# Weights that stand still: products of 512 and of 256 columns in turn, or in two groups

## The chip, the cores and the metric

The kernel runs on one core of a Trainium2 chip. Its time is the device time of that core in microseconds (us). The core has five engines that run side by side and wait for one another through semaphores: TensorE (matrix products; PE in the profile, its weight loads PEld), VectorE (DVE), ScalarE (ACT), GpSimd (POOL) and SyncE (SP, which issues most transfers). A product on TensorE has a stationary operand of 128 x 128, which a weight load brings in, and a moving operand that streams past it, here 512 or 256 columns wide. The result is added up in a bank of PSUM, which holds 512 float32 columns.

## The reference

One layer of a hybrid block for 256 tokens, with a context of 256 more, model width 2048. Both token sets are normalised and modulated, and multiplied with one wide matrix `w_in` (2048 x 19456), whose columns are cut into the inputs of two branches and their gates:

```python
xn = rmsnorm(h, norm_gain[l]) * (1.0 + scale) + shift
cn = rmsnorm(hc, norm_gain[l]) * (1.0 + scale_c) + shift_c
aq, ak, av, ag, hq, hff, hfb, hi, hg, ma, mb = split_columns(xn @ w_in[l])
```

The attention branch uses aq, ak, av with the context's keys and values and is gated by `silu(ag)`. The other branch is a gated recurrence over time in two directions: hff and hfb give its forget gates (also for the context, which gives the states to start from), hq its queries (through silu), hi its values, hg its output gate. Both are projected (`w_o_hgrn`, `w_o_attn`), merged with sigmoid gates from ma and mb, projected by `w_out`, added to x and normalised. All of it is float32.

## The kernel before

Each float32 factor is split into a high part, rounded to TensorE's float32r, and a low part, the remainder. A product of two such numbers is taken as high x high + high x low + low x high, three products on TensorE.

The weights come in chunks of 128 x 1024. SyncE transfers a chunk into `raw`, ScalarE makes the high part `wh` from it (L85, or L635 in the quad stage), VectorE the low part `wl` (L86, L636). `wh` and `wl` have three buffers each. In two places the weights are the stationary operand and the tokens move:

- `quad_col` (L639 to L685) computes the forget gates' columns for x and context. It is run 13 times and saves work by seven products of combined blocks in place of eight: `combos` forms combinations of four weight blocks on VectorE (L616), `token_sums` has formed those of the tokens (S) before. Each of the seven makes one chunk: eight products with the high part of the weights, whose moving operand is 512 columns, the high and the low part of the tokens side by side (L660), and then eight with the low part of the weights and 256 columns, the high part of the tokens (L663). All sixteen go into one bank; the low products add to its first 256 columns. A copy or a sum by ScalarE and VectorE (L667 to L679) takes the bank's content out behind the sixteenth.
- `proj_col_x_g` (L147 to L159) computes 256 columns for x alone (the recurrence's queries, the attention's gates). It goes through the 2048 rows in four chunks. A chunk has again eight products of 512 columns with the weights' high part (L154), then eight of 256 columns with the low part (L157), in turn over two banks. It is run 16 times: 64 chunks.

Everywhere else on this path (L100 to L103, L732 to L737) the tokens are stationary and the weights move.

TensorE's order is the order of the code in both stages (`manual_schedule`). The other engines' orders are set by a planner with modelled times, within the priorities that the code gives; the splits and the copies out of the banks have a high one. Around `proj_col_x_g`, the function `weave` lays the steps of the recurrence (`pair`) on TensorE between the chunks; it counts the columns that each chunk reports.

Of the kernel before, what the change touches and what calls it, by code (L numbers as in the profile page):

```python
# [16 lines left out]
T = 256  # L17
KT = D // P
# [20 lines left out]
def block_kernel(ctx: ExitStack, tc: tile.TileContext, x, c, cx, c_ctx, w_ada, b_ada, norm_gain, w_in,  # L39
                 b_merge, lb_f, lb_b, hg_gain, w_oh, sink, w_oa, w_out, fin_gain, cst, msk, out):  # L40
    nc = tc.nc
    pe, act, dve, pool = nc.tensor, nc.scalar, nc.vector, nc.gpsimd
# [18 lines left out]
    def wload(w, row0, nk, col0, ncol, rp=None):  # L61

        raw = (rp or wp).tile([P, 1024], F32, tag="raw", name="raw", bufs=8 if rp else 5)
        rv = raw[:, : len(col0) * nk * ncol].rearrange("p (g k c) -> p g k c", g=len(col0), k=nk)
        for g, co in enumerate(col0):
            nc.sync.dma_start(rv[:, g], w[row0: row0 + nk * P, co: co + ncol].rearrange("(k p) c -> p k c", p=P))
        return raw, rv
# [10 lines left out]
    def wchunk(w, row0, nk, col0, ncol):  # L78
        cl = col0 if isinstance(col0, tuple) else (col0,)
        raw, rv = wload(w, row0, nk, cl, ncol)  # L80
        h = wp.tile([P, 1024], F32R, tag="wh", name="wh", bufs=3)
        lo = wp.tile([P, 1024], F32R, tag="wl", name="wl", bufs=3)
        n = len(cl) * nk * ncol
        with tc.high_priority(PRIO):
            last_hi[0] = act.activation(h[:, :n], raw[:, :n], AF.Copy).ins  # L85
            last_lo[0] = dve.tensor_tensor(lo[:, :n], raw[:, :n], h[:, :n].bitcast(F32), op=ALU.subtract).ins  # L86
        parts = [(h[:, g * nk * ncol: (g + 1) * nk * ncol].rearrange("p (k c) -> p k c", k=nk),
                  lo[:, g * nk * ncol: (g + 1) * nk * ncol].rearrange("p (k c) -> p k c", k=nk)) for g in range(len(cl))]
        return parts if isinstance(col0, tuple) else parts[0]
# [15 lines left out]
    def bank(name="pj"):  # L105
        return pj.tile([P, 512], F32, tag="pj", name=name)

    def proj_tok_g(w, col0, src, toks):
# [7 lines left out]
            yield len(toks) * 6 * 512  # L116
        return banks

    def result(g):

        while True:
            try:
                next(g)
            except StopIteration as e:
                return e.value

    def proj_tok(*a):
        return result(proj_tok_g(*a))
# [18 lines left out]
    def proj_col_x_g(w, col0):  # L147

        banks = [bank() for _ in range(2)]
        for k0 in range(0, KT, 4):  # L150
            h, lo = wchunk(w, k0 * P, 4, col0, 256)
            parts = [(banks[i], slice(i * P, (i + 1) * P), j) for j in range(4) for i in range(2)]
            for o, cs_, j in parts:
                pe.matmul(o.rearrange("p (a t) -> p a t", a=2), h[:, j, cs_], xHL[:, :, k0 + j, :T],  # L154
                          start=k0 + j == 0, stop=False)
            for o, cs_, j in parts:
                pe.matmul(o[:, :T], lo[:, j, cs_], xH[:, k0 + j, :T], start=False, stop=k0 + j == KT - 1)  # L157
            yield 24 * T
        return banks  # L159

# [16 lines left out]
    xHL = base.tile([P, 2, KT, 512], F32R, tag="xHL", name="xHL")  # L177
    xH, xL = xHL[:, 0], xHL[:, 1]
# [60 lines left out]
    with pl("st", reuse_waits="tile") as st:  # L239
# [153 lines left out]
        def first_highs(u, n):  # L393

            tg, nb = FIRST[u % 3]
            f = [wp.tile([P, 1024], F32R, tag=tg_, name=tg_, bufs=3)[:, : n * 512] for tg_ in ("wh", "wl")]
            qt = fp.tile([P, 2, 512], F32R, tag=tg, name="wq", bufs=nb)
            q = [qt[:, r, : n * 256] for r in range(2)]
            for hl, raw in zip((f, q), raws[u]):
                act.activation(hl[0], raw, AF.Copy)  # L400
            fv = [a.rearrange("p (k c) -> p k c", k=n) for a in f]
            chunks[u] = [[a[:, :, :256] for a in fv], [a.rearrange("p (k c) -> p k c", k=n) for a in q],
                         [a[:, :, 256:] for a in fv]]
            return [lambda hl=hl, raw=raw: dve.tensor_tensor(hl[1], raw, hl[0].bitcast(F32), op=ALU.subtract)
                    for hl, raw in zip((f, q), raws[u])]
# [54 lines left out]
        with tc.manual_schedule(engines={mybir.EngineType.PE, mybir.EngineType.SP, mybir.EngineType.Activation,  # L460
                                         mybir.EngineType.DVE}):
            unit = modulation(*UNITS[0])
            for i in range(4):
                rest(8)
                take(unit, 1)
                if i == 1:
# [6 lines left out]
            first = [(bank(), bank()), (bank(), bank()),  # L473
                     tuple(ps.tile([P, 512], F32, tag=tg, name="pf") for tg in ("o", "al2"))]

            plan = {0: 2, 2: 3, 3: 9}
            for u, (k, n) in enumerate(UNITS):
                lows = first_highs(u, n)
# [26 lines left out]
    def bank8():  # L505

        i = turn8[0] % 8
        turn8[0] += 1
        return bank() if i < 4 else ps.tile([P, 512], F32, tag=("tp", "o", "al1", "al2")[i - 4], name="pm")

    def half(a, h):

        return a.rearrange("p (a h t) -> p a h t", a=2, h=2)[:, :, h, :]

    def pairs_of(a):
        return a.rearrange("p (a t) -> p a t", a=2)
# [44 lines left out]
    with pl("sp", reuse_waits="tile") as sp:  # L561
# [49 lines left out]
        def combos(b):  # L611


            def sub(o, x_, y_):
                with tc.high_priority(PRIO):
                    dve.tensor_tensor(o, x_, y_, op=ALU.subtract)  # L616

            t = tmp()
            yield b["11"]
            sub(t, b["12"], b["11"])  # L620
            yield t
            sub(t, b["22"], t)
            yield t
            yield b["22"]
            sub(b["12"], b["22"], b["12"])
            yield b["12"]
            yield b["21"]
            sub(t, b["21"], t)
            yield t
# [9 lines left out]
        def quad_col(d, h0):  # L639

            co = (C_FF, C_FB)[d] + h0 * HD
            b = {n: wload(w_in, 1024 * (n[0] == "2"), 8, (co + HD * (n[1] == "2"),), HD)[0]
                 for n in ("11", "12", "22", "21")}
            m_ = [bank8() for _ in range(3)]
            into = {0: (0, True), 1: (1, True), 2: (0, False), 3: (1, False), 4: (0, False), 5: (2, True), 6: (0, False)}
            sg = [base.tile([P, 512], F32, tag="sm", name="sg", bufs=3) for _ in range(2)]
            s15 = fp.tile([P, 2, 512], F32, tag="F1", name="s15")
            su = None

            def joined(m, s, dst):  # L650


                dve.tensor_tensor(s, m, s, op=ALU.add)
                dve.tensor_tensor(dst, pairs_of(s[:, :T]), pairs_of(s[:, T:]), op=ALU.add)

            for (i, _, mv), src in zip(ORDER, combos(b)):
                h, lo = [a.rearrange("p (k c) -> p k c", k=8) for a in two(src)]
                z, fresh = into[i]
                for k in range(8):
                    pe.matmul(m_[z].rearrange("p (z a t) -> p z a t", z=2, a=2), h[:, k, :], mv(k),  # L660
                              start=fresh and k == 0, stop=False, skip_group_check=True)
                for k in range(8):
                    pe.matmul(pairs_of(m_[z][:, :T]), lo[:, k, :], mv(k)[:, 0], start=False, stop=k == 7,  # L663
                              skip_group_check=True)
                with tc.high_priority(2 * PRIO):
                    if i < 2:
                        act.activation(s15[:, i, :], m_[i], AF.Copy)  # L667
                    elif i == 2:
                        su = base.tile([P, 512], F32, tag="bb", name="su", bufs=2)
                        act.activation(su, m_[0], AF.Copy)  # L670
                    elif i == 3:
                        joined(m_[1], su, half(sg[1], 0))
                    elif i == 4:
                        joined(m_[0], s15[:, 1, :], half(sg[1], 1))
                    elif i == 5:
                        joined(m_[2], s15[:, 0, :], half(sg[0], 0))
                    else:
                        act.activation(half(sg[0], 1), pairs_of(m_[0][:, T:]), AF.Copy)
                        dve.tensor_tensor(half(sg[0], 1), pairs_of(m_[0][:, :T]), half(sg[0], 1), op=ALU.add)  # L679
            F = fp.tile([P, 2, 512], F32, tag="F0", name="F0", bufs=2)  # L680
            for i in (1, 0):
                act.activation(sg[i], sg[i], AF.Sigmoid)
                act.activation(F[:, i, :], sg[i], AF.Identity, scale=lbc[:, 2 + d, h0 + i: h0 + i + 1],
                               bias=lbc[:, d, h0 + i: h0 + i + 1])
            nc.scalar.dma_start(F_dr[d][h0 // 2], F.rearrange("p i t -> p (i t)"))  # L685
# [774 lines left out]
    for n in range(3):  # L1460
        bo = [bank() for _ in range(2)]
        for k0 in range(0, KT, 2):
            h, lo = wchunk(w_out, k0 * P, 2, n * 512, 512)
# [8 lines left out]
    for k0 in range(0, KT, 4):  # L1472
        h, lo = wchunk(w_out, k0 * P, 4, D - 512, 256)
# [85 lines left out]
```

## Time and profile before

| | |
|---|---|
| median of 3 runs | 1584.49 us (1583.45 to 1588.19) |
| profiled execution | 1586.59 us, its span 1584.8 us |
| TensorE busy | 1561.6 us, 99% of the span |
| VectorE busy | 1201.5 us, 76% |
| ScalarE busy | 860.5 us, 54% |
| GpSimd busy | 142.1 us, 9% |
| granted TensorE clock | 0.999 |
| products, and weight loads | 10954 each |
| quad stage (`quad_col`) | from 440 to 699 us |
| woven stage (`proj_col_x_g` among others) | from 695 to 1252 us |

Times in the views are microseconds from the span's start, unless marked ns. A row of the timeline has the start, the time from the first start to the last end, the engine, the line of the code, the operation, the tiles it writes and reads, and how many instructions were merged. A row of the groups has the count, the busy time, the mean of one in ns, and the idle time before them. Ends of products on TensorE are modelled and overlap the next one's start, so that paces are read from starts. A row of the waits says who waited for whom, the total, how often, and the longest. A row of the chain of waits has the start, the time that it held the chain, and what it was.

### The profile page before, as it was taken

How to read it: one execution, taken by the hardware profiler on the slowest of the kernel's cores; microseconds unless marked ns; L12 is line 12 of the kernel's file. 1: busy time of each engine (PE TensorE's matmuls, PEld its weight loads, DVE VectorE, ACT ScalarE, POOL GpSimd, SP SyncE). 2: the span in 40 equal slices, each digit the busy share in tenths (PEclk: the TensorE clock that was granted, in tenths of full speed). 3: DMA queues.
4: the chain of work that ended last, by engine and by line, in shares of the span. 5: the costliest groups of instructions: out<-in, count | busy, mean ns of one | idle time of the engine just before them, and what ended most of it. 6: DMA issues, size and time to landing. Idle time of an engine off the chain costs nothing. (4 is left out here: it accounts for less than half of the span.)

```text
span 1584.8 us, 27868 instructions
## 1 busy us (share of the span) xinstructions
PE 1561.6 (99%) x10954; PEld 1343.8 (85%) x10954; DVE 1201.5 (76%) x1764; ACT 860.5 (54%) x1344; POOL 142.1 (9%) x280
## 2 busy tenths in 40 slices
PE   7999999999999999999999999999999999999998
PEld 4568899999988888888888888888888888888887
DVE  4449977777787878878888897888878777757764
ACT  4336443333355555566656666575666776744442
POOL 2000000000000000011212222121121000000000
PEclk9999999999999999999999999999999999999999
DMA  9996734434444444467777877878677854458661
GB/s 366 386 387 230 226 111 130 134 132 134 133 147 127 134 130 137 136 225 252 243 247 244 300 260 233 270 243 273 221 261 249 289 159 154 155 180 295 226 197 69
DMA packets 242900, 333.83 MB, mean 211 GB/s; under 512 B 12080, under 2 KB 162000, under 8 KB 242000
## 3 DMA queue, kind: packets, MB, share of 16 engines
q1 hardware_dynamic: 214096, 249.54, 48.5%
q0 software_dynamic: 19168, 64.08, 11.8%
q10 hardware_dynamic: 9504, 18.42, 3.2%
q8 instruction: 86, 1.41, 0.4%
q14 instruction: 46, 0.38, 0.1%
HBM read 300.53 MB, written 31.47 MB: 209 GB/s over the span
## 5 line engine op out<-in xcount | busy, mean ns | idle before, releaser
L85 ACT ACTIVATE wh<-raw 128x1024 fp32r<-128x1024 f32 x284 | 298.8, 1059 | 236.3 <-PE pj L101 151.7
L86 DVE TENSOR_TENSOR wl<-raw,wh 128x1024 fp32r<-128x1024 f32 x284 | 344.0, 1219 | 89.9 <-ACT wh L85 88.9
L100 PE MATMUL pj<-wh,xHL 128*128 128x512 f32 (+1 forms) x768 | 298.6, 390 | 0.0
L101 PE MATMUL pj<-wh,xHL 128*128 128x512 f32 (+1 forms) x768 | 294.8, 385 | 0.0
L103 PE MATMUL pj<-wl,xHL 128*128 128x512 f32 (+1 forms) x768 | 202.7, 385 | 0.0
L635 ACT ACTIVATE wh<-T 128x1024 fp32r<-128x1024 f32 x75 | 79.5, 1060 | 166.8 <-DVE T L616 83.9
L100 PEld LDWEIGHTS pj<-wh,xHL 128*128 128x128 f32 x768 | 144.4, 188 | 28.2 <-ACT sg L219 0.6
L101 PEld LDWEIGHTS pj<-wh,xHL 128*128 128x128 f32 x768 | 144.5, 188 | 27.6
L103 PEld LDWEIGHTS pj<-wl,xHL 128*128 128x128 f32 x768 | 142.0, 188 | 28.9
L635 ACT ACTIVATE wh<-raw 128x1024 fp32r<-128x1024 f32 x100 | 105.3, 1055 | 71.9 <-PE pj L734 23.7
L154 PE MATMUL pj<-xHL,wh 128*128 128x512 f32 x512 | 130.3, 396 | 0.0
L636 DVE TENSOR_TENSOR wl<-raw,wh 128x1024 fp32r<-128x1024 f32 x100 | 121.8, 1218 | 9.8 <-ACT wh L635 9.7
L636 DVE TENSOR_TENSOR wl<-T,wh 128x1024 fp32r<-128x1024 f32 x75 | 91.5, 1220 | 32.8 <-ACT wh L635 32.8
L154 PEld LDWEIGHTS pj<-xHL,wh 128*128 128x128 f32 x512 | 92.4, 189 | 16.9
L157 PEld LDWEIGHTS pj<-xHL,wl 128*128 128x128 f32 x512 | 69.8, 190 | 5.2
L204 DVE SCALAR_TENSOR_TENSOR acc<-hgw,cg,acc 128x512 f32<-128x512 f32 x60 | 44.9, 748 | 35.0 <-DMA hgw<-in_w_ada_dram 35.0
L157 PE MATMUL pj<-xHL,wl 128*128 128x256 f32 x512 | 71.3, 282 | 0.0
L912 DVE TENSOR_TENSOR A<-A,X 128x512 f32<-128x512 f32 x96 | 61.6, 682 | 0.1
L616 DVE TENSOR_TENSOR T<-raw,T 128x1024 f32<-128x1024 f32 x50 | 60.9, 1218 | 0.1
L616 DVE TENSOR_TENSOR raw<-raw 128x1024 f32<-128x1024 f32 x25 | 30.6, 1225 | 36.7 <-DMA raw<-in_w_in_dram 36.7
L541 POOL DMA_DIRECT2D hgw<-in_w_ada_dram x64 | 35.0, 547 | 235.3 <-DVE acc L204 157.6
L660 PE MATMUL pj<-S,wh 128*128 128x512 f32 x208 | 52.6, 395 | 1.6 <-ACT s L667 1.6
(353 smaller groups left out, 3155.1 us busy)
## 6 DMA issues: line engine op xcount, KB each, us to landing
raw<-in_w_in_dram SPq DMA_DIRECT2D x300, 512.0 KB, 4.6
raw<-in_w_ada_dram SPq DMA_DIRECT2D x64, 512.0 KB, 8.0
hgw<-in_w_ada_dram POOLq DMA_DIRECT2D x64, 256.0 KB, 4.5
raw<-in_w_o_hgrn_dram SPq DMA_DIRECT2D x32, 512.0 KB, 3.6
raw<-in_w_o_attn_dram SPq DMA_DIRECT2D x32, 512.0 KB, 4.1
raw<-in_w_out_dram SPq DMA_DIRECT2D x28, 512.0 KB, 4.1
F<-F POOLq DMA_DIRECT2D x16, 512.0 KB, 7.2
F<-F ACTq DMA_DIRECT2D x13, 512.0 KB, 4.4
```

The costliest lines, as they stand in the source:

```text
L85: last_hi[0] = act.activation(h[:, :n], raw[:, :n], AF.Copy).ins
L86: last_lo[0] = dve.tensor_tensor(lo[:, :n], raw[:, :n], h[:, :n].bitcast(F32), op=ALU.subtract).ins
L100: pe.matmul(o, s[0], m[0], start=first, stop=False)
L101: pe.matmul(o, s[1], m[0], start=False, stop=False)
L103: pe.matmul(o, s[0], m[1], start=False, stop=last)
L154: pe.matmul(o.rearrange("p (a t) -> p a t", a=2), h[:, j, cs_], xHL[:, :, k0 + j, :T], start=k0 + j == 0, stop=False)
L157: pe.matmul(o[:, :T], lo[:, j, cs_], xH[:, k0 + j, :T], start=False, stop=k0 + j == KT - 1)
L616: dve.tensor_tensor(o, x_, y_, op=ALU.subtract)
L635: act.activation(h, src, AF.Copy)
L636: dve.tensor_tensor(lo, src, h.bitcast(F32), op=ALU.subtract)
L660: pe.matmul(m_[z].rearrange("p (z a t) -> p z a t", z=2, a=2), h[:, k, :], mv(k), start=fresh and k == 0, stop=False, skip_group_check=True)
L912: dve.tensor_tensor(av, av, f.unsqueeze(3).to_broadcast([P, 2, n2, b]), op=ALU.mult)
```

## The change

Both places issue the same products with the same operands into the same banks. Their order within a chunk is another: a new function `in_turn` puts a few high products first (four in `proj_col_x_g`, three in `quad_col`), then a low and a high in turn until the highs are used up, then the lows that are left. For three first the order of the sixteen is HHH LH LH LH LH LH LLL.

```diff
+    def in_turn(highs, lows, lead):
+
+        order = [highs.pop(0) for _ in range(lead)]
+        for hi, lo in zip(highs, lows):
+            order += [lo, hi]
+        return order + lows[len(highs):]
+
@@ proj_col_x_g
             parts = [(banks[i], slice(i * P, (i + 1) * P), j) for j in range(4) for i in range(2)]
-            for o, cs_, j in parts:
-                pe.matmul(o.rearrange("p (a t) -> p a t", a=2), h[:, j, cs_], xHL[:, :, k0 + j, :T],
-                          start=k0 + j == 0, stop=False)
-            for o, cs_, j in parts:
-                pe.matmul(o[:, :T], lo[:, j, cs_], xH[:, k0 + j, :T], start=False, stop=k0 + j == KT - 1)
+            highs = [(o.rearrange("p (a t) -> p a t", a=2), h[:, j, cs_], xHL[:, :, k0 + j, :T], k0 + j == 0, False)
+                     for o, cs_, j in parts]
+            lows = [(o[:, :T], lo[:, j, cs_], xH[:, k0 + j, :T], False, k0 + j == KT - 1) for o, cs_, j in parts]
+            for o, w_, m, first, last in in_turn(highs, lows, 4):
+                pe.matmul(o, w_, m, start=first, stop=last, skip_group_check=True)
             yield 24 * T
@@ quad_col
-                for k in range(8):
-                    pe.matmul(m_[z].rearrange("p (z a t) -> p z a t", z=2, a=2), h[:, k, :], mv(k),
-                              start=fresh and k == 0, stop=False, skip_group_check=True)
-                for k in range(8):
-                    pe.matmul(pairs_of(m_[z][:, :T]), lo[:, k, :], mv(k)[:, 0], start=False, stop=k == 7,
-                              skip_group_check=True)
+                highs = [(m_[z].rearrange("p (z a t) -> p z a t", z=2, a=2), h[:, k, :], mv(k), fresh and k == 0, False)
+                         for k in range(8)]
+                lows = [(pairs_of(m_[z][:, :T]), lo[:, k, :], mv(k)[:, 0], False, k == 7) for k in range(8)]
+                for o, w_, m, first, last in in_turn(highs, lows, 3):
+                    pe.matmul(o, w_, m, start=first, stop=last, skip_group_check=True)
```

A high is a product with the weights' high part and 512 columns, a low one with their low part and 256 columns.

## The prediction, on record before the changed kernel ran

> **What bounds the kernel now.** I read the page first, for the engines' shares.
>
> ```profile
> span 1584.8 us, 27868 instructions
> ...
> PE 1561.6 (99%) x10954; PEld 1343.8 (85%) x10954; DVE 1201.5 (76%) x1764; ACT 860.5 (54%) x1344; POOL 142.1 (9%) x280
> ...
> L154 PE MATMUL pj<-xHL,wh 128*128 128x512 f32 x512 | 130.3, 396 | 0.0
> ...
> L157 PE MATMUL pj<-xHL,wl 128*128 128x256 f32 x512 | 71.3, 282 | 0.0
> ```
>
> TensorE is busy for 99% of the span, so what counts is the pace at which it takes its products. The change touches L154/L157 (512 products each) and L660/L663. How many of the latter there are, the groups kept apart by shape tell:
>
> ```profile
> L660 PE MATMUL pj<-S,wh 128*128 128x512 f32 x208 | 52.6, 395 | 1.6 <-ACT s L667 1.6
> L660 PE MATMUL pm<-S,wh 128*128 128x512 f32 x208 | 52.5, 394 | 0.7 <-ACT s L667 0.7
> L660 PE MATMUL pj<-xHL,wh 128*128 128x512 f32 x160 | 40.1, 392 | 0.0
> L660 PE MATMUL pm<-xHL,wh 128*128 128x512 f32 x152 | 38.0, 392 | 0.0
> ```
>
> That makes 728 = 91 chunks of 8 highs (512 columns) and 8 lows (256 columns), beside 64 chunks of L154/L157. The durations in these rows (about 395 and 282 ns) overlap and are no pace. The pace comes from starts, so next I took TensorE's timeline. Five whole chunks of the quad stage, first and last row:
>
> ```profile
> 487.83 2.00 PE L660 MATMUL pj<-S,wh 128*128 128x512 f32 x8
> ...
> 501.80 0.40 PE L660 MATMUL pm<-S,wh 128*128 128x512 f32 x1
> ```
>
> A chunk takes 13.97 / 5 = 2.794 us, so the 155 chunks take 433 us, 27% of the span. A difference of 0.3% of the run (4.75 us, about what a measurement of this kernel can tell from no change) would need 0.031 us per chunk.
>
> What would a chunk take if each product ran at its steady pace? For 512 columns I take a stretch that has only these (24 products lie between the two starts), for 256 columns likewise (24 again):
>
> ```profile
> 1454.68 0.39 PE L100 MATMUL pj<-wh,xHL 128*128 128x512 f32 x1
> ...
> 1460.12 0.39 PE L100 MATMUL pj<-wh,xHL 128*128 128x512 f32 x1
> ```
> ```profile
> 399.80 0.28 PE L732 MATMUL pj<-wh,xHL 128*128 128x256 f32 x1
> ...
> 402.68 0.28 PE L732 MATMUL pm<-wh,S 128*128 128x256 f32 x1
> ```
>
> That is 5.44 / 24 = 0.2267 us and 2.88 / 24 = 0.120 us. Eight of each make 2.773 us; the chunk of today is 0.021 us above that. The chain of waits shows where the surplus sits:
>
> ```profile
> 893.06 1.81 PE pj L154 x8
> 894.87 0.95 PE pj L157 x8
> 895.83 1.84 PE pj L154 x8
> ```
>
> The first eight highs follow other products of 512 columns and take 1.81; the next eight follow lows and take 1.84. Turning from lows back to highs thus costs about 0.02 to 0.03 us, once per chunk, and nothing else in the chunk is lost: no wait stands there.
>
> **The change part by part.** The same 16 products per chunk are issued, with the same weight loads, no DMA, no copy, no new tile. What moves is the order: quad chunks go HHH, then five times LH, then LLL; L154 chunks go HHHH, four times LH, LLLL. There are four things to price.
>
> *First, the loads.* Each product loads its own weights. If the loads of the lows set their pace, mixing in the highs would hide them. Products of 128 columns show the pace of loads, since they have half as much to stream:
>
> ```profile
> 920.00 1.88 PEld L946 LDWEIGHTS sb<-v,X 128*128 128x128 f32 x16
> 921.79 1.23 PEld L154 LDWEIGHTS pj<-xHL,wh 128*128 128x128 f32 x6
> ```
>
> Sixteen loads in 1.79 us, 0.112 each; a low at 0.120 is above this. So a load already fits behind a low, and the lows offer nothing that a high could hide. I price this part at nothing; the cover is the 0.008 us between 0.112 and 0.120. The Trainium skill has a rule that speaks against the change more bluntly: in "TensorE: Matmul & The Clock Gate", Part 3, section "The mechanism", it says that weight loads overlap running matmuls only where the row groups differ. All loads here use all rows, so by it load and stream would add up in any order and the sum would be zero as well; the trace disagrees with it, because the 0.19 us records of the loads fit into a pace of 0.12.
>
> *Second, the switches.* A quad chunk has six turns from lows to highs where it had one, the others five: 5 x 91 + 4 x 64 = 711 more. The trace has one place where a single high stands between lows, at the border of the two stages:
>
> ```profile
> 698.59 1.12 PE L663 MATMUL pm<-xHL,wl 128*128 128x256 f32 x8
> 699.54 0.40 PE L154 MATMUL pj<-xHL,wh 128*128 128x512 f32 x1
> 699.78 1.12 PE L157 MATMUL pj<-xHL,wl 128*128 128x256 f32 x8
> 700.74 2.00 PE L154 MATMUL pj<-xHL,wh 128*128 128x512 f32 x8
> 702.35 0.77 PEld L157 LDWEIGHTS pj<-xHL,wl 128*128 128x128 f32 x5
> 702.58 0.64 PE L157 MATMUL pj<-xHL,wl 128*128 128x256 f32 x4
> ```
>
> From 698.59 to 700.74 there are 16 lows and one high: 2.15 us, and at steady paces 16 x 0.120 + 0.227 = 2.147. The lone high costs nothing by itself. Up to 702.58 eight highs are added: 3.99 us against 3.960 at steady paces, 0.03 too much where one switch would make 0.02. So the lone switch costs between 0 and 0.01 us. At 0.01 the change loses 711 x 0.01 = 7.1 us. At 0, the surplus of 0.021 stays once per chunk (three or four lows at the tail, then three or four highs) and the sum is 0, or it vanishes because the highs never come eight in a row behind lows, and the sum is -155 x 0.021 = -3.3 us. I take -0.5 us: the lone high is the nearest row and speaks for 0 or slightly above, the possible relief of the long runs outweighs that a little. The ends for the range are -3.3 and +7.1.
>
> *Third, the wait of the first low moves forward.* The low part comes from VectorE; its first low now stands behind three or four highs, not eight, and behind it in TensorE's order stand the remaining highs, which a late low part would now hold up too. The tightest quad chunk that I found, with the load-to-load times beside VectorE's:
>
> ```profile
> 491.94 1.22 DVE L636 TENSOR_TENSOR wl<-raw,wh 128x1024 fp32r<-128x1024 f32 x1
> ...
> 492.66 1.06 ACT L635 ACTIVATE wh<-raw 128x1024 fp32r<-128x1024 f32 x1 [1.73 <-PE pj L660]
> ...
> 493.42 1.55 PE L660 MATMUL pj<-xHL,wh 128*128 128x512 f32 x6
> ```
>
> The low part ends at 493.16; the chunk's highs start at 493.42, and after two of them, at 493.87, the load of the first low is due. That leaves 0.71 us. Of the L154 chunks the tightest is this one:
>
> ```profile
> 831.43 1.22 DVE L86 TENSOR_TENSOR wl<-raw,wh 128x1024 fp32r<-128x1024 f32 x1 [5.21 <-ACT wh L85]
> ...
> 832.00 2.09 PE L154 MATMUL pj<-xHL,wh 128*128 128x512 f32 x8
> ...
> 833.70 0.42 PEld L157 LDWEIGHTS pj<-xHL,wl 128*128 128x128 f32 x2
> ```
>
> Its low part ends at 832.65; the load was due at 833.70 and will be at about 832.0 + 0.31 + 2 x 0.23 = 832.77 (the group's 2.09 is 0.09 more than the usual 2.00, which I put on its first high: 0.31). That leaves 0.1 us, once. Price: nothing; without that cover some tenths of a us.
>
> *Fourth, the high part's buffer comes free later.* The last high ends 8 x 0.227 + 5 x 0.120 = 2.41 us into a quad chunk (now 1.84) and 2.29 into the others: ScalarE's next split starts 0.57 or 0.45 us later. In the row above it starts at 492.66, right behind TensorE, and ends at 493.72; with three buffers its chunk comes three after the one that just gave it up, whose highs began 2.79 before 493.42: at 490.63 + 3 x 2.79 = 499.0. More than five us of cover, less 0.57. Nothing again. VectorE's part follows it, with the same cover, and the copies out of the banks still wait for the last low.
>
> *Sum:* 0 - 0.5 + 0 + 0 = -0.5 us. The profiled execution took 1586.59 us, 1.8 around its span of 1584.8; it would take 1586.1. It lies 2.1 above the median of the runs shown (1584.49), so for the median I say **1584.0 us**.
>
> **The rivals.**
>
> *Lows at the stream's pace (faster).* 512 columns take 0.2267, so half as many would take 0.113 if a low paid for its columns alone, and the 0.007 above that could be something that a high in between absorbs. Six lows of a quad chunk and five of the others would then stand behind a high: (6 x 91 + 5 x 64) x 0.007 = 6.1 us, with the surplus gone too (3.3) in all -9.4: 1575.1. For it: the first eight lows in the chain take 0.95, a little under 8 x 0.120. Against it: a load takes 0.112, so the next high's load would have to fit into a low of 0.113 exactly, and the lone high with 16 lows did not run faster. The skill's page "TensorE: Matmul & The Clock Gate" (opening table) lets the engine pull loads ahead of running matmuls within a 64-deep window, which would favour this rival. The trace has them ahead by one product only: in the border rows the load of the five lows starts at 702.35, 0.23 before their first product, which is one high.
>
> *Every switch pays in full (slower).* If the 0.021 is a fixed toll for turning from lows to highs, it is paid 711 times more: +14.9 us, 1599.4. It decides from 0.0067 us per switch on (4.75 / 711). For it: all chunks behind lows show 1.84. Against it: the lone high.
>
> *The other engines' order (slower).* ScalarE's and VectorE's order is planned from modelled times, which the change moves. Waits by TensorE's lines, two rows:
>
> ```profile
> PE pj L660 <- ACT s L667: 1.6, 1, 1.6
> ...
> PE pm L660 <- ACT s L667: 0.7, 1, 0.7
> ```
>
> Two stalls, 1.6 and 0.7 us, one each, for a copy out of a bank (L667) that came late on ScalarE: two of the 91 / 7 = 13 quads have one. In the other eleven at their mean of 1.15 it would be +12.7: 1597.2; if both vanish, -2.3. Speaking against it: TensorE's order is written out by hand and the copy's place has not changed.
>
> *The change doesn't do what it says:* the order of TensorE's products is written out by hand in both places, so I give this nothing.
>
> **How the numbers follow.** Forecast (between -3.3 and +7.1): 0.63, of which 0.05 lie above +4.75. Lows at the stream's pace: 0.20. Every switch in full: 0.10. Order of the others: 0.07, of which 0.05 slower and 0.02 within. Faster: 0.20. Slower: 0.05 + 0.10 + 0.05 = 0.20. The rest, 0.58 + 0.02 = 0.60, is no change that can be told. The likeliest case alone spans 1581.2 to 1591.6. The range takes in the faster rival, at 1575, and reaches upward to 1594, half way to the fixed toll; beyond it lie full tolls and many stalls.
>
> **What would show it.** In the profile after, TensorE's timeline of a quad chunk, start to start, is to take 2.77 to 2.80 us. Under 2.74 the lows ran at 0.113; at 2.87 or more the toll is paid at each turn. L660 and L663 rows should show no new releaser beyond ScalarE's L667, and no wait on VectorE's low part (L636, L86) should appear in front of a weight load; one at every chunk would prove my third step wrong. ScalarE's wait for TensorE before its splits should grow without TensorE's idle time growing. If the chunks keep their pace and the time still moves by more than 5 us, the cause is outside them and my forecast wrong for a reason that it does not hold.

## The result: slower by 1.6%, and not by the pace of the products

The changed kernel took 1612.58 us (median of 5 executions, 1609.15 to 1615.24), the kernel before 1586.23 us beside it. The ratio is 1.0164, with a 95% interval of 1.0146 to 1.0183, which is 26 us. The prediction was 1584.0 us, with a range up to 1594, so it was wrong. The profiled execution took 1609.15 us, 22.6 more than the one of before. In the medians here and below two executions are left out as slow, one of e9 (1924.53 us, granted clock 0.753) and one of the kernel before beside e13 (5506.51 us).

In the changed code the lines have moved: the products of the quad stage, L660 and L663 before, are L670; L154 and L157 are L164; the combinations of weight blocks, L616, are L623; the splits, L635 and L636, are L642 and L643; the copies out of the first two banks, L667, are L673; the store of the gates, L685, is L691.

From the page of the changed kernel, the span and two groups:

```profile
span 1607.3 us, 27847 instructions
...
L670 PE MATMUL pj<-S,wh 128*128 128x512 f32 x208 | 72.5, 415 | 11.6 <-ACT s L673 11.6
...
L623 DVE TENSOR_TENSOR raw<-raw 128x1024 f32<-128x1024 f32 x25 | 30.6, 1226 | 51.9 <-DMA raw<-in_w_in_dram 51.9
```

The waits of TensorE in the changed kernel:

```profile
PE pj L670 <- ACT s L673: 11.6, 6, 2.4
...
PE pm L670 <- ACT s L673: 3.1, 5, 2.0
```

Eleven waits for a copy out of a bank, 14.7 us, where there were two with 2.3 us. First I asked whether the chunks had kept their pace. The timeline of TensorE in the changed kernel, first rows of chunks, two of the quad stage and two of the woven stage:

```profile
519.55 0.86 PE L670 MATMUL pm<-xHL,wh 128*128 128x512 f32 x3
...
522.34 0.85 PE L670 MATMUL pj<-xHL,wh 128*128 128x512 f32 x3
...
722.23 1.09 PE L164 MATMUL pj<-xHL,wh 128*128 128x512 f32 x4
...
725.04 1.09 PE L164 MATMUL pj<-xHL,wh 128*128 128x512 f32 x4
```

From start to start it is 2.79 and 2.81 us. Between the waits, then, the sixteen products take what they took, to within 0.02 us. What has grown is the time from quad to quad (a quad is one run of `quad_col`, seven chunks). Two of these copies come per quad; the second one of the third and of the twelfth quad, before:

```profile
486.45 0.58 ACT L667 ACTIVATE s<-pj 128x512 f32<-128x512 f32 x1
...
665.83 0.58 ACT L667 ACTIVATE s<-pm 128x512 f32<-128x512 f32 x1
```

and after:

```profile
489.27 0.58 ACT L673 ACTIVATE s<-pj 128x512 f32<-128x512 f32 x1
...
685.65 0.58 ACT L673 ACTIVATE s<-pm 128x512 f32<-128x512 f32 x1
```

Nine quads take 179.38 us before, 19.93 each, and 196.38 after, 21.82 each. Seven chunks at 2.793 are 19.55. Eleven quads, as many as wait, at 1.89 us more would make 20.8 us. Measured on TensorE, the first 90 chunks of the stage take 255.0 us before (440.12 to 695.16) and 276.2 after (440.46 to 716.64), 21.1 more. That is nearly the whole difference of the profiled executions.

What sets 21.82 us? The four weight blocks of a quad are called 11, 12, 22 and 21. The first combination is 12 - 11, the second is 22 minus the first, the third is 22 - 12, and the fourth is 21 minus the second. I followed one quad round, from its first copy backward to what it waited for. Timeline of the kernel before, all engines (start, length, engine, line):

```profile
520.55 1.23 DVE L616 TENSOR_TENSOR T<-raw 128x1024 f32<-128x1024 f32 x1 [0.55 <-DMA raw<-in_w_in_dram]
...
521.69 1.22 DVE L616 TENSOR_TENSOR T<-raw,T 128x1024 f32<-128x1024 f32 x1
...
522.95 1.06 ACT L635 ACTIVATE wh<-T 128x1024 fp32r<-128x1024 f32 x1 [1.93 <-DVE T L616]
...
525.38 0.58 ACT L667 ACTIVATE s<-pm 128x512 f32<-128x512 f32 x1
...
526.02 2.08 PE L660 MATMUL pm<-S,wh 128*128 128x512 f32 x8
...
526.43 10.47 SPq L66 DMA_DIRECT2D raw<-in_w_in_dram  x4
...
527.64 0.33 ACTq L685 DMA_DIRECT2D F<-F  x1
...
530.11 1.23 DVE L616 TENSOR_TENSOR raw<-raw 128x1024 f32<-128x1024 f32 x1 [1.44 <-DMA raw<-in_w_in_dram]
...
535.29 1.22 DVE L636 TENSOR_TENSOR wl<-raw,wh 128x1024 fp32r<-128x1024 f32 x1
...
536.53 0.37 SPq L66 DMA_DIRECT2D raw<-in_w_in_dram  x1
...
540.16 1.23 DVE L616 TENSOR_TENSOR T<-raw 128x1024 f32<-128x1024 f32 x1 [0.53 <-DMA raw<-in_w_in_dram]
```

The same of the changed kernel:

```profile
504.04 1.23 DVE L623 TENSOR_TENSOR T<-raw 128x1024 f32<-128x1024 f32 x1 [1.00 <-DMA raw<-in_w_in_dram]
...
506.44 1.06 ACT L642 ACTIVATE wh<-T 128x1024 fp32r<-128x1024 f32 x1 [3.98 <-DVE T L623]
...
508.87 0.57 ACT L673 ACTIVATE s<-pj 128x512 f32<-128x512 f32 x1
...
509.49 0.53 PEld L670 LDWEIGHTS pj<-S,wh 128*128 128x128 f32 x3 [2.06 <-ACT s L673]
...
509.92 22.23 SPq L66 DMA_DIRECT2D raw<-in_w_in_dram  x5
...
510.18 0.33 ACTq L691 DMA_DIRECT2D F<-F  x1
...
515.44 1.23 DVE L623 TENSOR_TENSOR raw<-raw 128x1024 f32<-128x1024 f32 x1 [3.09 <-DMA raw<-in_w_in_dram]
...
520.63 0.42 DVE L661 TENSOR_TENSOR sg<-s 128x256 f32<-128x256 f32 x1
...
520.98 1.22 DVE L643 TENSOR_TENSOR wl<-raw,wh 128x1024 fp32r<-128x1024 f32 x1
...
522.22 0.37 SPq L66 DMA_DIRECT2D raw<-in_w_in_dram  x1
...
525.91 1.23 DVE L623 TENSOR_TENSOR T<-raw 128x1024 f32<-128x1024 f32 x1 [1.08 <-DMA raw<-in_w_in_dram]
```

These rows form a loop. On VectorE the first combination of the *next* quad (`T<-raw`) stands ahead of the second combination of this quad (`T<-raw,T`). It waits for the transfer of the next quad's block 12, and all behind it waits with it: the second combination, the third split (`wh<-T`), and on ScalarE the copy behind that split. A little later a low part frees a `raw` buffer, and SyncE issues the transfer of the next quad's block 22 into it (526.43, 509.92). The third combination (`raw<-raw`), of the next quad too, waits for that. From it VectorE works without a gap to the low part of the next quad's first chunk (535.29, 520.98), which frees a buffer for block 12 of the quad after that (536.53, 522.22), whose landing starts the loop anew.

| piece of the loop, us | before | after | more |
|---|---|---|---|
| first combination to the load of block 22 | 5.88 | 5.88 | 0 |
| that load to the third combination | 3.68 | 5.52 | 1.84 |
| third combination to the load of block 12 | 6.42 | 6.78 | 0.36 |
| that load to the next first combination | 3.63 | 3.69 | 0.06 |
| sum | 19.61 | 21.87 | 2.26 |

Before, this loop was as long as TensorE's work on a quad (19.55); the copy ended at 525.96, and the chunk that needs its bank started at 526.02. After, it is 2.26 us longer, and TensorE waits for the copy in eleven of the thirteen quads.

Two pieces grew. The larger: 1.21 us after the load of block 22 ScalarE sent the store of the gates (`F<-F`, 512 KB), and in the changed kernel it sends it 0.26 us after. The smaller: on VectorE the second sums (L661) now run ahead of the low parts. Both are a matter of order. From the programs of the two kernels, in the order of each engine (the quad's own steps; ' marks those of the next quad; sum a adds a bank to what was copied before, L653 or L660, and sum b is the second sum behind it, L654 or L661):

```
ScalarE, before:  ... split 1'  split 2'  sigmoid  gate ... split 4'  sigmoid  copy 1'  split 5'  gate  copy 2'
ScalarE, after:   ... split 1'  sigmoid  gate  split 2' ... split 4'  sigmoid  copy 1'  gate  split 5'  copy 2'
VectorE, before:  sum a  low 7  sum b  sum a  low 1'  sum b  sum a  low 2'  sum b
VectorE, after:   sum a  sum b  low 7  sum a  sum b  low 1'  sum a  sum b  low 2'
```

### The profile page after: what moved, and what is told of

It reads as the page before. It is cut to its first block, busy times and chain, and to the rows that moved or that the text cites. A ratio compares the mean times of both kernels' runs of the same rounds, so it can differ in the third digit from the quotient of the medians.

```text
span 1607.3 us, 27847 instructions
## 1 busy us (share of the span) xinstructions
PE 1572.5 (98%) x10954; PEld 1348.9 (84%) x10954; DVE 1205.7 (75%) x1764; ACT 860.5 (54%) x1344; POOL 141.7 (9%) x280
## 3 DMA queue, kind: packets, MB, share of 16 engines
q0 software_dynamic: 19168, 64.08, 11.5%
## 5 line engine op out<-in xcount | busy, mean ns | idle before, releaser
L642 ACT ACTIVATE wh<-T 128x1024 fp32r<-128x1024 f32 x75 | 79.4, 1058 | 161.1 <-DVE T L623 98.5
L164 PE MATMUL pj<-xHL,wh 128*128 128x512 f32 x512 | 161.1, 398 | 0.0
L642 ACT ACTIVATE wh<-raw 128x1024 fp32r<-128x1024 f32 x100 | 105.3, 1054 | 85.1 <-PE pj L740 21.9
L643 DVE TENSOR_TENSOR wl<-raw,wh 128x1024 fp32r<-128x1024 f32 x100 | 121.9, 1219 | 11.5 <-ACT wh L642 10.4
L643 DVE TENSOR_TENSOR wl<-T,wh 128x1024 fp32r<-128x1024 f32 x75 | 91.7, 1222 | 34.7 <-ACT wh L642 34.6
L164 PE MATMUL pj<-xHL,wl 128*128 128x256 f32 x512 | 112.5, 281 | 0.0
L164 PEld LDWEIGHTS pj<-xHL,wh 128*128 128x128 f32 x512 | 92.3, 188 | 17.5
L164 PEld LDWEIGHTS pj<-xHL,wl 128*128 128x128 f32 x512 | 87.6, 189 | 5.7
L670 PE MATMUL pj<-S,wh 128*128 128x512 f32 x208 | 72.5, 415 | 11.6 <-ACT s L673 11.6
L670 PE MATMUL pm<-S,wh 128*128 128x512 f32 x208 | 69.9, 405 | 3.1 <-ACT s L673 3.1
L623 DVE TENSOR_TENSOR raw<-raw 128x1024 f32<-128x1024 f32 x25 | 30.6, 1226 | 51.9 <-DMA raw<-in_w_in_dram 51.9
L623 DVE TENSOR_TENSOR T<-raw,T 128x1024 f32<-128x1024 f32 x50 | 60.9, 1219 | 0.1
```

The costliest lines, as they stand in the source:

```text
L164: pe.matmul(o, w_, m, start=first, stop=last, skip_group_check=True)
L642: act.activation(h, src, AF.Copy)
L643: dve.tensor_tensor(lo, src, h.bitcast(F32), op=ALU.subtract)
L670: pe.matmul(o, w_, m, start=first, stop=last, skip_group_check=True)
```

## The experiments

Every kernel here computes the whole layer. The quads' time in the text is that of nine quads, from the second copy of the third quad to that of the twelfth, divided by nine; the load is that of block 22, from issue to landing, a median over eleven quads, in us like the two columns beside it.

| kernel | median, us | ratio, 95% | a quad | waits for copies | load | store behind the load's issue |
|---|---|---|---|---|---|---|
| before | 1586.23 | | 19.93 | 2.3 | 3.8 | 1.21 |
| after (three first, in turn) | 1612.58 | 1.0146 to 1.0183 | 21.82 | 14.7 | 5.5 | 0.26 |
| e1_x_only | 1589.04 | 0.9996 to 1.0022 | 19.82 | 0.5 | 3.8 | 1.21 |
| e2_lead4 | 1607.09 | 1.0104 to 1.0149 | 21.57 | 11.5 | 5.5 | 0.26 |
| e3_swapped | 1594.84 | 1.0038 to 1.0065 | 20.48 | 6.8 | 3.8 | 1.21 |
| e4_copy_first | 1594.77 | 1.0033 to 1.0070 | 20.26 | 0 | 4.1 | 0.74 ahead |
| e5_store_early | 1603.70 | 1.0089 to 1.0126 | 21.54 | 13.9 | 5.5 | 0.26 |
| e6_turn4_store_late | 1590.24 | 1.0002 to 1.0028 | 19.92 | 1.0 | 3.7 | 5.0 |
| e7_turn3_store_late | 1594.47 | 1.0033 to 1.0067 | 20.27 | 4.0 | 3.7 | 5.1 |
| e8_old_store_late | 1587.98 | 0.9993 to 1.0012 | 19.81 | 0.8 | 3.6 | 4.5 |
| e9_turn3_first_sum | 1588.08 | 0.9995 to 1.0013 | 19.62 | 0 | 4.2 | 0.82 |
| e10_turn3_pinned | 1594.49 | 1.0025 to 1.0056 | 20.25 | 4.0 | 3.6 | 5.1 |
| e11_old_both | 1584.23 | 0.9969 to 0.9987 | 19.55 | 0 | 3.6 | 6.0 |
| e12_old_sum_ahead | 1584.01 | 0.9957 to 0.9981 | 19.55 | 0 | 3.6 | 6.0 |
| e13_turn3_sum_behind | 1592.34 | 1.0015 to 1.0038 | 20.11 | 2.0 | 3.7 | 5.1 |

Each ratio is against the kernel before on the same chip, which took 1586.48 (e1 to e4), 1587.86 (e5 to e8), 1587.72 (e9 to e11), 1587.33 (e12) and 1588.12 us (e13).

### Which part, and order or release

**e1_x_only** keeps the turns in `proj_col_x_g` and puts the groups back in `quad_col`. **e2_lead4** keeps both, with four highs first in the quads too:

```diff
-                for o, w_, m, first, last in in_turn(highs, lows, 3):
+                for o, w_, m, first, last in in_turn(highs, lows, 4):
```

> The turn-taking only in proj_col_x_g (64 chunks); quad_col as before. Theory O (the other order of ScalarE and VectorE in the quad stage makes the loss): within 2 us of before, as the woven stage of the changed kernel was only about 1 us longer. Theory P (turn-taking itself slows TensorE, in proportion to its chunks): 64/155 of the loss of 26 us, so +11 us. Theory R (the high part's buffer comes free too late): up to +8 us, since here too it comes free later, by 0.45 us.

> The changed kernel with four highs first in quad_col, not three. The planner then puts ScalarE's sigmoid of a quad behind the next quad's second split and VectorE's second sum (i = 3) behind the seventh split, as it did before the change; with three it put them ahead. Theory O: the loss goes, time within 4 us of before, one or two stalls of L673 left. Theory P: three turns in four still stand, so at least +15 us. Theory R: the buffer comes free 0.45 us later, not 0.57, so the loss shrinks by a fifth at most: +20 us.

e1 took the loss away: it belongs to the quad stage, and the 64 chunks of the woven stage cost too little to be told from nothing (2.6 us by the medians, an interval of -0.6 to +3.5). e2 gave back 6 of 26 us only. VectorE's order is there that of before, and ScalarE's differs from it in one place: the gate stands ahead of split 5. The load took 5.5 us again. So the smaller piece of the loop depends on three first, and the larger one doesn't. The loss that stayed, 20.6 us, is also what theory R had expected, the late release of the high part's buffer; e5 and e6 below decide between it and the order.

**e3_swapped** has the groups of before and is given the changed kernel's order of sums and of the first sigmoid; **e4_copy_first** is the changed kernel with the third split behind the copy out of the first bank:

```diff
@@ e3: each low part behind the second sum that ran ahead of it after the change
+                with tc.issue_after(la) if la is not None else ExitStack():
+                    dve.tensor_tensor(lo, src, h.bitcast(F32), op=ALU.subtract)
@@ e4
-                h, lo = [a.rearrange("p (k c) -> p k c", k=8) for a in two(src)]
+                h, lo = [a.rearrange("p (k c) -> p k c", k=8) for a in two(src, copied if i == 2 else None)]
```

> The kernel before, with its two groups, but ScalarE's and VectorE's order in the quad stage forced to that of the changed kernel: the second split of a quad behind the sigmoid and the gate of the quad before, and the seventh, first and second low parts behind the second sums for i = 3, 4 and 5. Theory O: +12 to +25 us, with ten or more stalls of TensorE on L667. Theories P and R: within 3 us of before, because TensorE's order and the release of the buffers are those of before.

> The changed kernel, with the third split of a quad forced behind the copy of its first bank (i = 0), so that the copy no longer stands behind a split that waits for a transfer. Theory O (with the copy's place as the point where TensorE is held): most of the loss goes, within 6 us of before; TensorE no longer waits for that copy, and what is left of the late transfers shows as short waits for the high or low part. Theory P: no gain, +20 us or more. Theory R: the waits move from the copy to the split, +10 to +20 us.

e3 lost 8 us, less than the 12 to 25 expected and not 26, with the products in groups: an order alone costs time, but these places are the smaller part of it. In e3 the gate stayed behind split 5, and the load took 3.8 us. e4 ended all waits for copies and gave back 18 us, yet it stayed 8 us above the kernel before where at most 6 were expected, and its quads still took 20.26 us. Its TensorE waits instead for high and low parts in the quads, seven times and 2.6 us in all, since the loop of the loads goes on behind the copy. The planner answered this edit too with another order: VectorE's third combination stands one low part later, and the store goes out ahead of the load.

### The store beside the load

What e2 kept and e3 lacked is the gate ahead of split 5, and so the store 0.26 us behind the load. **e5_store_early** puts that one thing into the kernel before, products in groups:

```diff
-                h, lo = [a.rearrange("p (k c) -> p k c", k=8) for a in two(src)]
+                h, lo = [a.rearrange("p (k c) -> p k c", k=8) for a in two(src, gate_of[0] if i == 4 else None)]
```

with the split issued behind `gate_of[0]`, the gate's last step. **e6_turn4_store_late**, **e7_turn3_store_late** and **e8_old_store_late** send the store behind the next quad's seventh split, with four highs first, with three first, and with the groups of before:

```diff
+                if i == 6 and unsent:
+                    with tc.issue_after(made[0]):
+                        nc.scalar.dma_start(*unsent.pop())
-            nc.scalar.dma_start(F_dr[d][h0 // 2], F.rearrange("p i t -> p (i t)"))
+            unsent.append((F_dr[d][h0 // 2], F.rearrange("p i t -> p (i t)")))
```

> The kernel before, with its two groups; only ScalarE's fifth split of a quad is forced behind the second gate of the quad before, so that the store of the gates goes out a ScalarE split earlier, about 0.26 us behind the load of the next quad's third weight block in place of 1.2 us. Theory S (the store meets that load, VectorE's combination stands waiting for it in order, and TensorE in the end): that load takes about 5.5 us in place of 3.7, TensorE waits for the copy of the first bank (L667) in most quads, +12 to +22 us in all, with nothing of TensorE's order changed. Theory R (the late release of the high part's buffer): within 3 us of before.

> The turn-taking in both places, four highs first in quad_col too, and the store of a quad's gates held back behind the seventh split of the next quad. Theory S: the load takes 3.7 us again, and the 20 us of the run with four highs first are gone: within 3 us of before. Theory R: nothing gained, +15 to +20 us.

> The changed kernel as it was (three highs first) with the store held back in the same way. Theory S: the load takes 3.7 us again; what is left is the loss of VectorE's and ScalarE's other order, as in the run that forced only this on the two groups: +3 to +10 us. Theory R: +20 us or more.

> The kernel before with the store held back. Theory S: the load never meets the store, so it takes 3.5 to 3.8 us; the two or three stalls of before go: 0 to -3 us. Theory R: no change, within 1 us.

e5's timeline, and its waits of TensorE below:

```profile
509.01 12.20 SPq L66 DMA_DIRECT2D raw<-in_w_in_dram  x4
...
509.27 0.33 ACTq L688 DMA_DIRECT2D F<-F  x1
...
514.65 1.23 DVE L616 TENSOR_TENSOR raw<-raw 128x1024 f32<-128x1024 f32 x1 [3.20 <-DMA raw<-in_w_in_dram]
```
```profile
PE pj L663 <- ACT s L670: 8.3, 6, 2.1
...
PE pm L663 <- ACT s L670: 5.6, 3, 2.7
```

Without a single product moved, the swap of one gate and one split costs 15.8 us: the third combination starts 5.64 us behind the load's issue. Where the store goes out late, the load takes 3.6 to 3.7 us, and with four highs first the loss is gone but for 2.4 us (e6). This is the larger piece. Theory R, which expected e5 within 3 us of before and no gain in e6, falls as an account of it. With three first 6.6 us stay (e7). In the kernel before a late store changes the time by nothing that can be told (e8).

### What stayed with three first

**e9_turn3_first_sum** is the changed kernel, its store still early, with one thing moved on VectorE: the next quad's first combination goes behind this quad's second one.

```diff
-            sub(t, b["12"], b["11"])
+            with tc.issue_after(second[0]) if second[0] is not None else ExitStack():
+                sub(t, b["12"], b["11"])
             yield t
-            sub(t, b["22"], t)
+            second[0] = sub(t, b["22"], t)
```

**e10_turn3_pinned** is e7 with the first sigmoid and its gate behind split 2' and the second sum of the fourth product behind low 7, as before the change. **e11_old_both** is e8 with the edit of e9.

> The changed kernel (three first, store not held back); VectorE's first combination for the next quad, which waits for a transfer of that quad's blocks, is forced behind the second combination of this quad, which needs no transfer and feeds TensorE two chunks later. Theory S with its last link (VectorE's order passes a late transfer on to this quad's work): the third load is still 5.5 us, but its lateness reaches TensorE less: half of the loss or more goes, +3 to +13 us. If the last link is wrong: +20 us or more.

> The changed kernel (three first) with the store held back and, beside this, the sigmoid of a quad queued behind the next quad's second split and the second sum for i = 3 behind the seventh low part, as they were before the change; the second sums for i = 4 and 5 stay ahead. Theory S and order: most of the 6.6 us that holding back the store had left is order, so +1 to +4 us. If instead the later release of the high part's buffer (0.57 us here) makes that rest: +5 to +8 us.

> The kernel before, its two groups kept, with the store held back and the first combination of the next quad behind the second of this one: the version that the theory offers against both kernels. Expected: no stall on L667 left, 1 to 3 us under before, and no more, as TensorE is busy nearly throughout. If the cover was not the point: no change.

e9 did more than expected. VectorE's two combinations in e9, and ScalarE's second copies of the third and the twelfth quad:

```profile
498.59 1.22 DVE L625 TENSOR_TENSOR T<-raw,T 128x1024 f32<-128x1024 f32 x1
499.73 1.22 DVE L625 TENSOR_TENSOR T<-raw 128x1024 f32<-128x1024 f32 x1
```
```profile
485.68 0.58 ACT L676 ACTIVATE s<-pj 128x512 f32<-128x512 f32 x1
...
662.22 0.58 ACT L676 ACTIVATE s<-pm 128x512 f32<-128x512 f32 x1
```

With the turns, the early sums and a store 0.82 us behind the load, a quad takes 176.54 / 9 = 19.62 us and waits for no copy. The loop is cut where the work of this quad stood behind a transfer for the next one. The edit brought a second change with it that I had not set: the planner then also put copy 1 ahead of the second sigmoid on ScalarE. e9 doesn't tell apart how much of the gain is the cut and how much this. In e11, below, the second sigmoid stays ahead of copy 1 and TensorE waits for no copy either, though there with groups and a late store.

e11 cuts the loop in the kernel before; the same two copies:

```profile
485.61 0.58 ACT L675 ACTIVATE s<-pj 128x512 f32<-128x512 f32 x1
...
661.59 0.59 ACT L675 ACTIVATE s<-pm 128x512 f32<-128x512 f32 x1
```

175.98 / 9 = 19.55 us, TensorE's own pace. The run is 0.22% faster than the kernel before, 3.5 us where 1 to 3 were expected. The loop, with the store beside it, had been costing that kernel its 0.38 us per quad.

e10 moved nothing against e7, and the reading that its two places hold the rest fell. Its 6.8 us lie in the range that it had given to the other reading, the later release of the buffer, so that one stayed in play. **e12_old_sum_ahead** and **e13_turn3_sum_behind** ask for one other place, the second sum of the fifth product, which stands ahead of low 1' after the change. e12 puts it ahead in e8; e13 puts it behind in e7, with the first sigmoid behind split 2' too:

```diff
@@ e12
-                h, lo = [a.rearrange("p (k c) -> p k c", k=8) for a in two(src)]
+                h, lo = [a.rearrange("p (k c) -> p k c", k=8) for a in two(src, summed[0] if i == 0 else None)]
@@ e13
-                dve.tensor_tensor(dst, pairs_of(s[:, :T]), pairs_of(s[:, T:]), op=ALU.add)
+                add = lambda: dve.tensor_tensor(dst, pairs_of(s[:, :T]), pairs_of(s[:, T:]), op=ALU.add)
+                late_add.append(add) if i == 4 else add()
@@ e13, behind the first split of the next quad
+                        with tc.high_priority(2 * PRIO), tc.issue_after(made[1]):
+                            late_add.pop()()
```

> The kernel before, its products in groups, with the store of the gates sent late, and with one order set on VectorE: the low part of a quad's first chunk waits behind the second sum of the fifth product of the quad before. (1) The order of the sums: this low part sets free the buffer into which block 12 is loaded, and that load ends in front of the first combination, on a loop that is as long as TensorE's work on a quad. 0.35 to 0.45 us more on the loop should give a stall of some 0.3 to 0.6 us on the copy out of the first bank in about eleven quads, 4 to 7 us in all against the kernel before: 1592 to 1595 if that takes 1587.7. (2) The later release in the turn-taking chunks is what cost the kernel with three highs first and a late store its 0.5%, and the order of the sums is harmless: then nothing changes here beside the same kernel without this order (within 1 us of the kernel before), and no more than two or three quads stall.

> Products in turn with three highs first, the store of the gates late, and the second sum of the fifth product behind the low part of the next quad's first chunk, as in the kernel before; the first combination of the next quad stays ahead of the second combination of this one. (1) The order of this one sum is what was left: the low part of the first chunk starts 0.4 us earlier behind the sum of block 22, the loop that holds the copy out of the first bank is as short as in the kernel before, and the stalls of the quads fall from 5.8 us to under 2.5: 0 to 2.5 us above the kernel before, 1588 to 1590 if that takes 1587.5. (2) The later release of the buffers in the turn-taking chunks, or another part of the order, is what was left: the eleven stalls of about half a us stay, and with them the 0.4 to 0.5%, 1594 to 1595.

e12 missed its expectation, since the planner answered it by putting the first combination of the next quad behind the second one as well. So it became a second e11, and like it ran at 19.55 us per quad, with the sum ahead: where the loop is cut, this order harms nothing. e13 is the cleaner test, for VectorE's order differs from e7's in that one sum. The third combination and the low part that frees the buffer, in e7:

```profile
510.10 1.23 DVE L623 TENSOR_TENSOR raw<-raw 128x1024 f32<-128x1024 f32 x1 [1.29 <-DMA raw<-in_w_in_dram]
...
515.72 1.22 DVE L645 TENSOR_TENSOR wl<-raw,wh 128x1024 fp32r<-128x1024 f32 x1
```

and in e13:

```profile
510.68 1.23 DVE L623 TENSOR_TENSOR raw<-raw 128x1024 f32<-128x1024 f32 x1 [1.21 <-DMA raw<-in_w_in_dram]
...
516.05 1.23 DVE L645 TENSOR_TENSOR wl<-raw,wh 128x1024 fp32r<-128x1024 f32 x1
```

5.62 us became 5.37 (5.18 before the change). The waits for copies fell from eleven with 4.0 us to two with 2.0, a quad from 20.27 to 20.11 us, and the run from 6.6 to 4.2 us above the kernel before. The direction is that of the first reading, the time short of it (0 to 2.5 were expected). The 0.19 us left on that piece may belong to the sum of the fourth product, still ahead of low 7 in e13; restored without the other (e10) it brought nothing, and both together weren't tried. What else holds the 4.2 us stays open; the later release of the buffer is among what could.

## Why the prediction was wrong

**First step, the loads (nothing).** Nothing speaks against it: no chunk got shorter.

**Second step, the switches (-3.3 to +7.1, taken -0.5).** The mechanism was right, the size a little off. In e9 and e11 no quad waits for a copy, and a quad takes 19.62 us in turn and 19.55 in groups: 0.01 us per chunk, 0.9 us in thirteen quads. In the woven stage, chunks that follow one another directly take 2.812 us after, in the median, and 2.794 before, which is 1.2 us over 64 chunks. That makes 2 us by the traces. The medians of e9 and e11, against the same runs of the kernel before, lie 3.9 us apart, and e1 alone gave 2.6 with an interval that takes in zero. All of these lie inside the bounds, on the other side of zero from the value I took. The rivals that priced each switch, downward to 1575.1 or upward to 1599.4, are both out: the chunks at 2.79 and 2.81 lie between their 2.74 and 2.87.

**Third step, the wait of the first low (nothing).** It held. No wait for VectorE's low part stands in front of these products after the change.

**Fourth step, the buffer that comes free later ("Nothing again").** This is the step that failed. In place of nothing, the copies out of the banks came late in eleven quads and the stage took 21.1 us more, because the loop they hang on had gone from 19.61 to 21.87 us. I checked the cover of the splits, more than five us, and wrote that "the copies out of the banks still wait for the last low". I didn't ask for the copy's own cover, which was 0.06 us, and didn't follow the copy backward: it stood behind the third split, that behind a combination, and that behind a transfer. Nor did I follow what a later release does to orders that a planner makes from modelled times. Since TensorE's order is all that the change moves in the code, the other engines' orders flipped through those times. Which of the times decided is argued here and wasn't traced. Where the loop keeps its length or is cut, the later release costs little: e6 and e9 have it too, and their quads take 19.92 and 19.62 us.

**The rival of the other engines' order (0.07, 1597.2).** It had the side and the place right and the count nearly: it thought of stalls for the copy in all thirteen quads, and eleven came. It had the price of one at 1.15 us where the waits took 1.34 on average and a quad lost 1.89, and no mechanism that would have told it so. I held against it that "the copy's place has not changed". It had not, and that proved nothing, because the copy was late through what stood ahead of it in three queues. Had I gone once round the loop in the timeline, I would have found it to be 19.61 us long beside TensorE's 19.55, with no cover at all for whatever the planner does next. That alone should have weighed more than 0.07.

The sentence that the cause lies outside the chunks "if the chunks keep their pace and the time still moves by more than 5 us" is what came.

## What to carry to other kernels

When an engine is busy 99% of the span, look for a loop through other engines and transfers that is just as long, and go round it once with start times: a cover of some hundredths of a us is none. A change to one engine's hand-written order can change every order that a planner makes from its times, so compare all engines' orders before arguing that the rest stays. An operation for the next stage that is hoisted ahead in a queue and waits for a transfer blocks everything of this stage behind it; put it behind the work that is ready.

## What was unexpected in the hardware

**A store slows a load by when it is issued.** In the medians of the table, a load of 512 KB landed after 3.6 to 3.7 us where the store of 512 KB was issued 4.5 us or more later, after 3.8 us at 1.21, 4.2 at 0.82, and 5.5 at 0.26 us. Where the store went out 0.74 us ahead (e4) it was 4.1. That the two come from different engines' queues didn't keep them apart. The Trainium skill says so in "DMA: Bandwidth & Descriptors", section "Issuing engines are not separate DMA queues": transfers started by any engine run on the same 16 DMA engines and interleave. The traces agree, in that a store from ScalarE's queue slows a load from SyncE's. The page gives no figure for what the one costs the other; here it was up to 1.8 us.

**A halved clock that cost almost nothing.** Stretches of the changed kernel, with the granted clock in the column behind the engines:

```profile
507.00:510.60 3.60, 1.74 (x10) 1.35 (x9) 3.07 (x3) 3.60 (x6) 0.00 (x0) 1.00 0.01 2
510.60:514.00 3.40, 3.40 (x13) 2.95 (x13) 1.65 (x2) 1.51 (x3) 0.00 (x0) 0.50 0.74 248
514.00:517.50 3.50, 3.50 (x21) 3.00 (x20) 2.06 (x2) 1.90 (x3) 0.00 (x0) 1.00 0.71 211
```

After the wait of 2.06 us at 509.49 TensorE ran at half the clock for 3.4 us, and did 13 products there against 21 in the stretch behind it. That happened after four of the seven waits of about 2 us. The Trainium skill's "TensorE: Matmul & The Clock Gate", section "HAM oscillation — how this bites in real kernels", asks for no idle gap above some 3.4 us; here gaps of about 2 us were enough in some quads and not in others, while the length of the slow spells, 3.41 us each, agrees. In e2 and e5 all five waits of 2.1 to 2.9 us met such a spell, and none of the ten waits of 1.4 to 1.8 us did. I had first counted these spells as a loss of their own, 1.7 us each. They weren't. From wait to wait, the three quads that began with a spell took 21.6 to 21.9 us, those without one 21.7 to 22.2. The loop set the pace, and the wait behind a spell was 0.4 to 0.7 us where it was else about 2.
